# A two-block model on one core: the state space set-up with D's diagonal on TensorE and at even steps, and the state space mixer's matmuls grouped by kind

## Chip, core and metric

The kernel runs on one core of a Trainium2 chip. The metric is the device time in microseconds (us). TensorE (PE) multiplies, PEld is its weight load, VectorE (DVE), ScalarE (ACT) and GpSimd (POOL) do the rest, and SyncE (SP) issues most of the loads from HBM. ACT and POOL issue some DMAs as well, in order with their own instructions.

## What is computed

A model of two blocks on x [512 tokens, 1024 channels]. The change touches the second block: the state space mixer of its second layer, and the set-up of that mixer's factors, which is done during the feed-forward part of the layer before.

```python
# s5_mixer: 64 groups of 16 channels, each with 64 complex states
ab = exp(lr*dt) * (cos(li*dt) + 1j*sin(li*dt))       # per group and state
x[t] = ab * x[t-1] + bb @ u[t]                       # linear scan over 512 tokens
y[t] = Re(c @ x[t]) + d * u[t]                       # d: one number per channel
g_a, g_b = split(gelu(y) @ w_glu);  x_res += g_a * sigmoid(g_b)
# conv_ffn, once per layer
h = x @ w_up; h = conv_b + sum_j conv_w[j] * h[t-2+j]
x_res += (silu(h[:2816]) * h[2816:]) @ w_down
```

## The kernel before

Every large product is made of three matmuls of split fp32 operands: `lin` (L268 to L270) multiplies hi by wh, lo by wh and hi by wl. For each weight tile `wload` has SP load `w`, ACT round it to `wh` (L223) and DVE subtract to get `wl` (L224). There are three buffers of `w` and two each of `wh` and `wl`, so ACT must make the next `wh` while PE uses the present one.

**The feed-forward part, `ffn(l, ...)`.** Two halves. Each half has eleven pairs of products with w_up (loop over `j`; 24 matmuls each), whose results pass through DVE (L1995, L1999) and ACT (L1997, L2002), and then eight products with w_down (loop over `n`; 33 matmuls each). In layer 0 a generator, `s5_setup`, is advanced in between by `step(sg)`; in layer 1 there is nothing to advance. A Tile scheduler puts the instructions of each engine into order.

**The set-up, `s5_setup`.** Eight steps `q`, each for four pairs of groups, each in two parts. The first part is on POOL alone (`tt`, L1507): complex products that fill `s_bb`, `s_gr`, `s_gi`, `s_vr`, `s_vi` (512 and 576 elements per partition, two buffers each), two DMAs to `v_d`, and a table of 64 powers, `s_tab`, by six doublings of six instructions on 4 to 128 elements, sent to `tab_d` (one buffer). The second part has PE transpose `s_gr` and `s_gi` (L1570), which ACT copies to `s_w` and sends to `w_d`, and has PE multiply `s_bb` by `s_vr` and `s_vi` (L1583) into `sk`, which ACT copies to `s_k` (L1586). POOL then adds the diagonal that carries d, `s_owns` (made at L1576), to `s_k` (L1587), and ACT issues four DMAs of `s_k` to `k_d` (L1590).

**The mixer, `mixer3`.** Four steps `q` of sixteen groups. `blocks(q)` multiplies the inputs `U[q]` by `w` (from `w_d`) on PE (L1649); `states(...)` runs the scan on DVE (L1665 to L1675) with the table `tab` (from `tab_d`) and leaves `X`; `outputs(q, ...)` adds on PE, for each `e` of 8, the product of `U` with `tm` from `k_d` (L1697, all 128 rows of the array by 64 columns) and of `X` with `v` from `v_d` (L1701, 64 rows by 64 columns); `gelus` transposes (L1714) and applies the gelu. `U[0]` is first scaled by `rj` on DVE (L1642), `U[1]` to `U[3]` on POOL (L1725). `tm`, `v` and `w` share four buffers, tag `w5`, and `tab` has two; SP issues all their loads from `q` 2 on, in one queue (`factors`, L1685 and L1687, and `s5_load`, L1613 and L1615). PE's order here is that of the code. Then the products with `w_gl` begin.

## Time and profile before

| | |
|---|---|
| time, median of 3 runs | 2511.63 us (2510.29 to 2514.41) |
| the profiled execution: its time, its span | 2509.73 us, 2507.7 us |
| granted TensorE clock, mean over the span | 0.970 |
| busy: PE, DVE, ACT, POOL | 94%, 70%, 43%, 23% |
| POOL's busy time that lies within 1405 to 1830 us | 324.32 us |
| `ffn(0)` with the set-up, from its first L1995 to its last L2010 | 1457 to 1893 us |
| `mixer3` from its first L1649 to the first product with w_gl | 1946 to 2006 us |

All positions are microseconds from the span's start. A granted clock of 1.00 is 2.4 GHz and 0.50 is 1.2 GHz; a value between is a mean over a stretch. The two stretches in the last lines make up a fifth of the span, and PE is busy nearly all the time outside them.

### The profile page before, as it was taken

Reading aid. Unit: us, or ns where it says so; the run is one execution under the profiler, and the core shown is the slowest. Engines: PE = TensorE matmul, PEld = TensorE weight load, DVE = VectorE, ACT = ScalarE, POOL = GpSimd, SP = SyncE. Lnnn points to the kernel's source line nnn. Section 1 sums busy time; section 2 is a strip of 40 time slices with the busy share of each in tenths; the row PEclk is TensorE's granted clock in tenths of the full one; section 3 lists DMA queues with packets and bytes.
Section 4 is the critical chain, followed back from the end, with each engine's and each line's share of the span. In section 5 each row is a group of like instructions: output and inputs, shape, how many; then the busy total and the mean of one; then the engine's idle time right before and its main releaser. Section 6 shows DMA issues by size and latency. Waiting matters only on the chain.

```text
span 2507.7 us, 35944 instructions
## 1 busy us (share of the span) xinstructions
PE 2345.7 (94%) x13173; PEld 1909.4 (76%) x13174; DVE 1749.5 (70%) x3319; ACT 1088.4 (43%) x1706; POOL 564.5 (23%) x689
## 2 busy tenths in 40 slices
PE   7999899899999998899999987898999799999999
PEld 4666799677777776898767776686788588888887
DVE  6975668699996985777786766636657746755755
ACT  3444578434433434786345333323343234433432
POOL 0002344100000004443010599809800100000000
PEclk9999999899999998999999998998999899999999
DMA  9852688454353214896221333332346732323242
GB/s 345 294 193 88 244 316 314 166 179 133 112 176 134 97 63 144 294 334 235 88 68 62 92 112 103 104 109 97 109 145 196 208 105 93 98 85 110 94 122 97
DMA packets 136726, 385.94 MB, mean 154 GB/s; under 512 B 24632, under 2 KB 41144, under 8 KB 134496
## 3 DMA queue, kind: packets, MB, share of 16 engines
q1 hardware_dynamic: 121408, 338.51, 40.8%
q0 software_dynamic: 7488, 26.74, 3.2%
q10 hardware_dynamic: 7648, 18.32, 2.1%
q8 instruction: 108, 1.77, 0.3%
q14 instruction: 74, 0.61, 0.1%
HBM read 354.13 MB, written 29.38 MB: 153 GB/s over the span
## 4 chain that ended last, share of the span: by engine, by line
PE 35%; POOL 10%; DVE 4%; DMA 1%; issue 1%; ACT 1%; ACTq 0%; POOLq 0%; DVEq 0%; SPq 0%
PE ps L268 10%; PE ps L270 10%; PE ps L269 10%; POOL s_x L1507 3%; POOL s_tab L1507 2%; POOL s_gr L1507 1%; POOL s_gi L1507 1%; POOL s_vr L1507 1%; DVE wl L224 1%; DMA tab_d<-s_tab 1%; PE py L1701 1%; DMA w<-v_d 1%; POOL s_vi L1507 0%; POOL s_bb L1507 0%; POOL s_owns L1576 0%
## 5 line engine op out<-in xcount | busy, mean ns | idle before, releaser
L268 PE MATMUL ps<-hi,wh 128*128 128x512 f32 (+2 forms) x2248 | 903.0, 402 | 38.5 <-ACT wh L223 35.2
L270 PE MATMUL ps<-hi,wl 128*128 128x512 f32 (+2 forms) x2248 | 889.2, 396 | 9.4 <-DVE wl L224 9.4
L269 PE MATMUL ps<-lo,wh 128*128 128x512 f32 (+2 forms) x2248 | 888.0, 395 | 3.6 <-DVE lo L486 2.4
L223 ACT ACTIVATE wh<-w 128x1024 fp32r<-128x1024 f32 (+2 forms) x327 | 310.5, 951 | 620.6 <-PE ps L269 360.0
L224 DVE TENSOR_TENSOR wl<-w,wh 128x1024 fp32r<-128x1024 f32 (+3 forms) x323 | 368.3, 1140 | 275.0 <-ACT wh L223 270.8
L268 PEld LDWEIGHTS ps<-hi,wh 128*128 128x128 f32 (+1 forms) x2248 | 427.3, 190 | 144.7 <-ACT wh L223 39.2
L270 PEld LDWEIGHTS ps<-hi,wl 128*128 128x128 f32 (+1 forms) x2248 | 426.1, 190 | 114.3 <-DVE wl L224 17.8
L269 PEld LDWEIGHTS ps<-lo,wh 128*128 128x128 f32 (+1 forms) x2248 | 427.4, 190 | 97.7 <-DVE lo L486 4.4
L224 DVE TENSOR_TENSOR wl<-we,wh 128x1024 fp32r<-128x1024 f32 x128 | 169.3, 1338 | 64.8 <-ACT wh L223 60.3
L929 POOL TENSOR_TENSOR hl<-hT,hh 128x1024 fp32r<-128x1024 f32 x60 | 140.4, 2341 | 172.6 <-ACT hh L928 109.9
L223 ACT ACTIVATE wh<-we 128x1024 fp32r<-128x1024 f32 x128 | 135.3, 1059 | 52.4 <-DMA we<-in_w_ex_dram 23.0
L1999 DVE SCALAR_TENSOR_TENSOR hc<-f,cols,hc 128x511 f32<-128x511 f32 (+1 forms) x176 | 150.8, 857 | 7.0 <-ACT hc L1997 3.8
L909 PE MATMUL ps<-ht,w 128*128 128x128 f32 x1024 | 126.0, 276 | 6.7 <-ACT ht L959 6.6
L726 POOL IOTA io<- 128x512 f32 x2 | 1.1, 562 | 573.4 <-PE ps L270 573.4
L909 PEld LDWEIGHTS ps<-ht,w 128*128 128x128 f32 x1024 | 119.4, 191 | 9.4 <-ACT ht L959 9.2
L441 DVE CUSTOM_DVE_ANT_0 we<-we,crow 128x1024 f32<-128x1024 f32 x80 | 96.4, 1214 | 5.4 <-DMA we<-in_ada_t_dram 5.1
L1995 DVE TENSOR_TENSOR f<-ps,rb 128x512 f32<-128x512 f32 x88 | 60.4, 686 | 54.3 <-PE ps L270 54.0
L947 PE MATMUL pa<-wh,hh 128*128 128x256 f32 x496 | 89.3, 301 | 0.0
L223 ACT ACTIVATE hi<-hc 128x512 fp32r<-128x512 f32 x44 | 27.8, 632 | 128.4 <-DVE hc L2003 128.4
L491 DVE SCALAR_TENSOR_TENSOR x<-ps,mod,x 128x512 f32<-128x512 f32 x52 | 38.9, 748 | 59.1 <-PE ps L270 51.7
L947 PE MATMUL pa<-wl,hh 128*128 128x256 f32 x496 | 78.7, 281 | 1.5 <-DVE wl L224 1.5
L947 PE MATMUL pa<-wh,hl 128*128 128x256 f32 x496 | 79.2, 282 | 0.0
(570 smaller groups left out, 3331.0 us busy)
## 6 DMA issues: line engine op xcount, KB each, us to landing
we<-in_w_ex_dram SPq DMA_DIRECT2D x128, 512.0 KB, 6.0
w<-in_w_fu_dram SPq DMA_DIRECT2D x88, 512.0 KB, 3.5
we<-in_ada_t_dram SPq DMA_DIRECT2D x80, 512.0 KB, 5.1
w<-in_w_ex_dram SPq DMA_DIRECT2D x64, 512.0 KB, 5.6
w<-in_w_si_dram SPq DMA_DIRECT2D x48, 512.0 KB, 3.5
w<-in_w_fd_dram SPq DMA_DIRECT2D x32, 512.0 KB, 3.9
w<-in_w_ei_dram SPq DMA_DIRECT2D x20, 512.0 KB, 3.5
aw<-in_ada_w_dram SPq DMA_DIRECT2D x16, 512.0 KB, 9.1
```

The lines of the kernel that those rows point to most:

```text
L223: S.activation(hi, src, AF.Copy)
L224: eng.tensor_tensor(lo, src, hi.bitcast(F32), op=SUB)
L268: PE.matmul(ps[:m], a, h, start=(not more and k + j == 0), stop=False)
L269: PE.matmul(ps[:m], a, l, start=False, stop=False)
L270: PE.matmul(ps[:m], b, h, start=False, stop=(last and k + j == nk - 1))
L441: V.tensor_tensor_reduce(w, w, row, 1.0, 0.0, op0=MUL, op1=ADD, accum_out=st[:, n:n + 1])
L909: PE.matmul(p[:, c * 128:(c + 1) * 128], w2[:, (4 * q + c) * 128:(4 * q + c + 1) * 128], hd, start=True, stop=True)
L929: (V if e < 2 else G).tensor_tensor(hl_, win, hh.bitcast(F32), op=SUB)
L947: PE.matmul(hp[:, 0:256], h[:, 4 * n + k], w[:, k * 256:(k + 1) * 256], start=(n + i + k == 0), stop=(n + i + k == 6))
L1507: G.tensor_tensor(o, a, b, op=op)
L1995: V.tensor_tensor(t, next(up)[1], rb, op=MUL)
L1999: V.scalar_tensor_tensor(c[:, d:], t[:, :T - d], C(f"fw{l}{2 - d}", n), c[:, d:], op0=MUL, op1=ADD)
```

## The change

1. **D's diagonal.** `s_owns` is made once, for all steps, by one POOL instruction on 256 elements. PE adds it into `sk` by a product with the identity (16 columns), so ACT's copy to `s_k` is complete, and POOL's addition (L1587) is gone.
2. **Tables.** The doublings are done in the odd steps alone, for eight pairs of groups at once, on 8 to 256 elements. The third part of the table, `s_rr`, has its own tile and its own DMA in every step.
3. **Steps.** The generator is advanced once at `j` 0, twice at `j` 4 and 8 of each half, and twice after `n` 1 and 6 of each half's products with w_down, instead of at every `j` with remainder 0 or 2 by 3.
4. **Mixer.** The 16 products of `U` with `tm` of a step are made together in `within(q, tm)`, and the 32 products of `X` with `v` together in `outputs`. `within` stands ahead of the next `blocks`, and `factors` ahead of both, which moves the loads of `tm` and `v` ahead of those of `w` and `tab` on SP. The scaling of `U[1]` to `U[3]` on POOL is issued after DVE's scaling of `U[0]`.

```diff
+        owns = tl(ap, [128, 16, 16], "s_owns")
+        G.tensor_tensor(owns, own[:, None, :].to_broadcast([128, 16, 16]),
+                        C("sd", 0, 16)[:, :, None].to_broadcast([128, 16, 16]), op=MUL)
...
-            tb = tl(ap, [128, 3, 4, 64], "s_tab")
...
-            for b in range(6):
-                n = 1 << b
-                sh = [128, 4, n]
...
-            G.tensor_copy(tb[:, 2], mag[:, gq, None].to_broadcast([128, 4, 64]))
-            G.memset(tb[:, 2, :, 0:1], 0.0)
-            G.dma_start(tab_d[:, :, gq], tb)
+            if q % 2:
+                g2 = slice(4 * q - 4, 4 * q + 4)
+                tb = tl(ap, [128, 2, 8, 64], "s_tab")
...
+                for b in range(6):
+                    n = 1 << b
+                    sh = [128, 8, n]
...
+                G.dma_start(tab_d[:, 0:2, g2], tb)
+            rr = tl(ap, [128, 4, 64], "s_rr")
+            G.tensor_copy(rr, mag[:, gq, None].to_broadcast([128, 4, 64]))
+            G.memset(rr[:, :, 0:1], 0.0)
+            G.dma_start(tab_d[:, 2, gq], rr)
             yield
...
-            owns = tl(ap, [128, 2, 16], "s_owns", 2)
-            for ab in range(2):
-                G.tensor_scalar(owns[:, ab], own, C("sd", 2 * q + ab), 0.0, op0=MUL, op1=ADD)
...
-                                  m[pr, e, 0:8].rearrange("p m c -> p (m c)"), start=(a == 0), stop=(a == 1))
+                                  m[pr, e, 0:8].rearrange("p m c -> p (m c)"), start=(a == 0), stop=False)
+                PE.matmul(p[:, 0:16], ident, owns[:, 2 * q + ab], start=False, stop=True)
                 S.activation(k[:, ab], p[:, 0:128], AF.Copy)
-                G.tensor_tensor(k[:, ab, 0:16], k[:, ab, 0:16], owns[:, ab], op=ADD)
...
+            def within(q, tm):
+
+                ps = [ps_("py", 2) for _ in range(2)]
+                for e in range(8):
+                    for ab in range(2):
+                        PE.matmul(ps[e // 4][sides[ab], e % 4 * 128:e % 4 * 128 + 128], U[q][:, 8 * ab + e], tm[:, 8 * ab + e],
+                                  start=(e % 4 == 0), stop=False)
+                return ps
...
+                for h, p in enumerate(ps):
+                    for e in range(4 * h, 4 * h + 4):
+                        for a in range(2):
+                            for ab in range(2):
+                                PE.matmul(p[sides[ab], e % 4 * 128:e % 4 * 128 + 128], X[sides[ab], a, e],
+                                          v[sides[ab], e, a], start=False, stop=(a == 1 and e % 4 == 3))
...
             s0 = blocks(0)
-            for q in range(1, 4):
-                G.tensor_tensor(U[q], U[q], rj[:, None, :].to_broadcast([128, 16, 64]), op=MUL)
-            p0 = factors(0)
+            with tc.issue_after(scaled[-1]):
+                for q in range(1, 4):
+                    G.tensor_tensor(U[q], U[q], rj[:, None, :].to_broadcast([128, 16, 64]), op=MUL)
+            tm, v = factors(0)
+            X = states(*s0, gs=4)
+            y = within(0, tm)
             s1 = blocks(1)
-            X = states(*s0, gs=4)
-            o = outputs(*p0, X)
+            o = outputs(y, v, X)
             X = states(*s1)
             for q in range(2):
+                tm, v = factors(q + 1)
+                y = within(q + 1, tm)
                 s1 = blocks(q + 2)
-                p0 = factors(q + 1)
                 gelus(q, o)
-                o = outputs(*p0, X)
+                o = outputs(y, v, X)
                 X = states(*s1)
...
-                    if j % 3 == 0:
+                    if j == 0 or j % 11 in (4, 8):
                         step(sg)
-                    if j % 3 == 2 or j == 21:
-                        step(sg)
+                        if j % 11:
+                            step(sg)
...
+                    if n in (1, 6):
+                        step(sg, 2)
```

What the scheduler makes of it on ACT, at the third step of the set-up (before; `DVE`, `PE`, `Pool` and `Activation` in brackets are engines whose semaphores are waited for, `DMAHW` a load or store):

```order
L1586 ACTIVATE s_k<-sk 128x128 [waits DMAHW6_49,DMAHW1_49,DMAHW7_49,DMAHW0_49,PE_49]
L1573 DMA w_d<-s_w 128x1024 [waits Activation_49]
L1586 ACTIVATE s_k<-sk 128x128 [waits PE_49]
L223 ACTIVATE hi<-hc 128x512 [waits DVE_49]
L1590 DMA k_d<-s_k 16x2x128 [waits Pool_49]
L1590 DMA k_d<-s_k 16x2x128 x3
L223 ACTIVATE wh<-w 128x1024 [waits DMAHW5_49,PE_49]
```

And the same place of its second step after the change, where L1591 is the copy to `s_k`, L1580 the store to `w_d` and L1594 the store to `k_d`:

```order
L1591 ACTIVATE s_k<-sk 128x128 [waits DMAHW1_49,DMAHW2_49,DMAHW0_49,PE_49]
L1580 DMA w_d<-s_w 128x1024 [waits Activation_49]
L1591 ACTIVATE s_k<-sk 128x128 [waits PE_49]
L223 ACTIVATE hi<-hc 128x512 [waits DVE_49]
L1594 DMA k_d<-s_k 16x2x128 [waits Activation_49]
L1594 DMA k_d<-s_k 16x2x128 x3
L223 ACTIVATE wh<-w 128x1024 [waits DMAHW0_49,PE_49]
```

The stores stand where they stood, ahead of the next `wh`, but wait for ACT's own copy and no longer for POOL.

On PE, the first matmuls of the mixer before (U_19340 is `U[0]`, U_19348 `U[1]`, w_19449 `tm` and w_19458 `v` of step 0; a pair of the last two rows is one `e`):

```order
L1649 MATMUL ps<-U_19340,w_18931 64x64 x32
L1649 MATMUL ps<-U_19348,w_18935 64x64 x16
L1649 MATMUL pb<-U_19348,w_18935 64x64 x16
L1697 MATMUL py<-w_19449,U_19340 64x128 x2
L1701 MATMUL py<-w_19458,X 64x128 x4
L1697 MATMUL py<-w_19449,U_19340 64x128 x2
L1701 MATMUL py<-w_19458,X 64x128 x4
```

And after the change (L1655 is `blocks`, L1701 now `within`, L1712 `outputs`, L1724 the transposes; U_19174 is `U[0]`, U_19182 `U[1]`, U_19190 `U[2]`):

```order
L1655 MATMUL ps<-U_19174,w_18765 64x64 x32
L1701 MATMUL py<-w_19283,U_19174 64x128 x16
L1655 MATMUL ps<-U_19182,w_18769 64x64 x16
L1655 MATMUL pb<-U_19182,w_18769 64x64 x16
L1712 MATMUL py<-w_19292,X 64x128 x32
L1701 MATMUL py<-w_19435,U_19182 64x128 x16
L1655 MATMUL ps<-U_19190,w_19464 64x64 x32
L1724 MATMUL pm<-ident,o_19380 128x128 x8
L1712 MATMUL py<-w_19444,X 64x128 x32
```

What alternated eight times in a step now stands in one run of 16 and one of 32, and the run of 16 is ahead of the next `blocks`.

On SP, the loads for steps 1 and 2 of the mixer before (w_19601 is `w` of step 2, w_19639 `tm` and w_19648 `v` of step 1):

```order
L1613 DMA w_19601<-w_d 128x2048 [waits DMASW0_49,PE_49]
L1685 DMA w_19639<-k_d 16x16x128 [waits DMAHW1_49,DMASW2_49,PE_49]
L1615 DMA tab<-tab_d 128x3x512 [waits DMAHW2_49,DMASW1_49,DVE_49]
L1685 DMA w_19639<-k_d 16x16x128 x2
L1685 DMA w_19639<-k_d 16x16x128 [waits DMAHW5_49]
...
L1685 DMA w_19639<-k_d 16x16x128 [waits DMAHW1_49]
L1687 DMA w_19648<-v_d 128x2048 [waits DMAHW2_49,DMASW4_49,PE_49]
```

And after the change (L1691 loads `tm`, L1693 `v`, L1617 `w`, L1619 `tab`; w_19435 and w_19444 belong to step 1, w_19464 to step 2):

```order
L1691 DMA w_19435<-k_d 16x16x128 [waits DMAHW0_49,DMASW4_49,PE_49]
L1691 DMA w_19435<-k_d 16x16x128 [waits DMAHW1_49]
L1691 DMA w_19435<-k_d 16x16x128 x2
...
L1691 DMA w_19435<-k_d 16x16x128 [waits DMAHW7_49]
L1693 DMA w_19444<-v_d 128x2048 [waits DMAHW0_49,DMASW6_49,PE_49]
L1617 DMA w_19464<-w_d 128x2048 [waits DMAHW1_49,DMASW6_49,PE_49]
L1619 DMA tab<-tab_d 128x3x512 [waits DMAHW2_49,DMASW5_49,DVE_49]
```

The load of `tab`, which waits for DVE, stood ahead of seven of the eight loads of `tm` and of that of `v`; it stands behind them now.

## Rows read from the trace of the kernel before

**Rows 1.** Busy time by stretch; the third-last column is the granted clock.

```profile
1405.00:1600.00 195.00, 168.36 (x812) 133.91 (x810) 126.24 (x138) 68.31 (x95) 178.11 (x295) 0.94 0.34 105
...
1690.00:1830.00 140.00, 124.58 (x601) 99.44 (x600) 91.93 (x99) 50.19 (x73) 118.12 (x197) 0.90 0.34 108
1457.40:1893.40 436.00, 392.37 (x1889) 313.00 (x1888) 254.43 (x280) 149.07 (x212) 278.00 (x468) 0.94 0.36 111
2104.80:2457.40 352.60, 352.60 (x1560) 291.08 (x1559) 218.29 (x279) 141.65 (x179) 0.00 (x0) 1.00 0.33 102
```

**Rows 2.** Waits from 1405 to 1830: us in total, times, longest.

```profile
ACT wh L223 <- POOL s_x L1507: 65.8, 6, 14.9
...
PE ps L268 <- ACT wh L223: 35.2, 6, 10.8
```

**Rows 3.** ACT in order of time, at the third step: start, duration.

```profile
1584.61 0.28 ACT L1586 ACTIVATE s_k<-sk 128x128 f32<-128x128 f32 x1 [0.26 <-ACT s_k L1586]
...
1595.89 1.73 ACTq L1590 DMA_DIRECT2D k_d<-s_k  x4
1597.73 1.06 ACT L223 ACTIVATE wh<-w 128x1024 fp32r<-128x1024 f32 x1 [10.89 <-POOL s_x L1507]
```

**Rows 4.** POOL in order of time at the same step.

```profile
1595.63 0.22 POOL L1587 TENSOR_TENSOR s_k<-s_k,s_owns 128x16 f32<-128x16 f32 x1
```

**Rows 5.** ACT in order of time, at the seventh step.

```profile
1823.89 1.06 ACT L223 ACTIVATE wh<-w 128x1024 fp32r<-128x1024 f32 x1 [1.49 <-PE ps L269]
```

**Rows 6.** POOL's groups from 1400 to 1835; the last with its shapes apart.

```profile
L1507 POOL TENSOR_TENSOR s_x<-s_tab 128x4 f32<-128x4 f32 (+5 forms) x96 | 48.0, 500 | 6.8
L1507 POOL TENSOR_TENSOR s_tab<-s_tab 128x4 f32<-128x4 f32 (+5 forms) x96 | 41.5, 436 | 0.0
L1507 POOL TENSOR_TENSOR s_tab<-s_tab,s_x 128x4 f32<-128x4 f32 (+5 forms) x96 | 39.7, 414 | 1.2
...
L1576 POOL TENSOR_SCALAR s_owns<-s_own,cols 128x16 f32<-128x16 f32 x16 | 13.6, 861 | 0.1
...
L1507 POOL TENSOR_TENSOR s_tab<-s_tab 128x128 f32<-128x128 f32 x16 | 11.0, 688 | 0.0
```

**Rows 7.** The chain that ended last, at one step: start, duration, work.

```profile
1686.99 0.87 PE pm L1570 x8
1687.87 0.71 PE sk L1583 x32
```

**Rows 8.** The same chain in the mixer.

```profile
1962.06 5.46 DMA tab<-tab_d
1967.61 7.64 DMA w<-v_d
...
1990.52 0.58 PE py L1701 x8
1991.10 0.37 PE py L1697 x4
...
2006.24 0.43 PE ps L268
```

**Rows 9.** POOL, then DVE, in order of time as the mixer begins.

```profile
1945.52 7.93 POOL L1725 TENSOR_TENSOR U<-U,rj 128x1024 f32<-128x1024 f32 x3 [51.33 <-DVE rj L1635]
...
1945.47 3.44 DVE L1642 TENSOR_TENSOR U<-U,rj 128x512 f32<-128x512 f32 x2
...
1952.51 1.22 DVE L1667 TENSOR_TENSOR b<-b,f 128x256 f32<-128x256 f32 x1
```

**Rows 10.** DVE in order of time: ends of the scans of steps 1 and 3.

```profile
1970.82 1.26 DVE L1675 TENSOR_TENSOR X<-X,f 128x504 f32<-128x504 f32 x2
...
1985.63 0.69 DVE L1665 TENSOR_TENSOR b<-ps,tab 128x512 f32<-128x512 f32 x1 [0.96 <-PE ps L1649]
...
1996.06 1.27 DVE L1675 TENSOR_TENSOR X<-X,f 128x504 f32<-128x504 f32 x2
```

**Rows 11.** DMA issues from 1890 to 2010: KB each, median us to landing.

```profile
w<-w_d SPq DMA_DIRECT2D x2, 1024.0 KB, 9.5
```

More of the change, by code (lines that the diff above doesn't have):

```diff
@@ L1549, in s5_setup @@
                 G.dma_start(v_d[:, gq, a].rearrange("p g (m c) -> p g m c", c=16), v[:, :, 1:9])
-            tb = tl(ap, [128, 3, 4, 64], "s_tab")
-            xt = x.rearrange("p a b c -> p (a b c)").rearrange("p (a c) -> p a c", a=4)
-            G.tensor_copy(tb[:, 0, :, 0], uc[:, gq])
-            G.tensor_copy(tb[:, 1, :, 0], us[:, gq])
-            for b in range(6):
-                n = 1 << b
-                sh = [128, 4, n]
-                cmul(tb[:, 0, :, n:2 * n], tb[:, 1, :, n:2 * n], tb[:, 0, :, n - 1:n].to_broadcast(sh),
-                     tb[:, 1, :, n - 1:n].to_broadcast(sh), tb[:, 0, :, 0:n], tb[:, 1, :, 0:n], xt[:, :, 0:n])
-            G.tensor_copy(tb[:, 2], mag[:, gq, None].to_broadcast([128, 4, 64]))
-            G.memset(tb[:, 2, :, 0:1], 0.0)
-            G.dma_start(tab_d[:, :, gq], tb)
+            if q % 2:
+                g2 = slice(4 * q - 4, 4 * q + 4)
+                tb = tl(ap, [128, 2, 8, 64], "s_tab")
+                xt = x.rearrange("p a b c -> p (a b c)").rearrange("p (a c) -> p a c", a=8)
+                G.tensor_copy(tb[:, 0, :, 0], uc[:, g2])
+                G.tensor_copy(tb[:, 1, :, 0], us[:, g2])
+                for b in range(6):
+                    n = 1 << b
+                    sh = [128, 8, n]
+                    cmul(tb[:, 0, :, n:2 * n], tb[:, 1, :, n:2 * n], tb[:, 0, :, n - 1:n].to_broadcast(sh),
+                         tb[:, 1, :, n - 1:n].to_broadcast(sh), tb[:, 0, :, 0:n], tb[:, 1, :, 0:n], xt[:, :, 0:n])
+                G.dma_start(tab_d[:, 0:2, g2], tb)
[3 more added lines that the diff above has]
+            G.dma_start(tab_d[:, 2, gq], rr)
             yield
@@ L1635, in mixer3 @@
             V.tensor_copy(rj, rp[:, 0:64])
+            scaled = []
             def blocks(q):
@@ L1687, in factors, with outputs @@
                 nc.sync.dma_start(v, v_d[:, 8 * q:8 * q + 8])
-                return q, tm, v
-            def outputs(q, tm, v, X):
-                o = tl(bp, [128, 8, 8, 16], "o5", 2)
-                for e in range(8):
-                    if e % 4 == 0:
-                        p = ps_("py", 2)
-                    for ab in range(2):
-                        PE.matmul(p[sides[ab], e % 4 * 128:e % 4 * 128 + 128], U[q][:, 8 * ab + e], tm[:, 8 * ab + e],
-                                  start=True, stop=False)
-                    for a in range(2):
-                        for ab in range(2):
-                            PE.matmul(p[sides[ab], e % 4 * 128:e % 4 * 128 + 128], X[sides[ab], a, e],
-                                      v[sides[ab], e, a], start=False, stop=(a == 1))
-                    if e % 4 == 3:
-                        S.activation(o[:, :, e - 3:e + 1].rearrange("p t e c -> p e t c"),
-                                     p.rearrange("p (e t c) -> p e t c", e=4, t=8), AF.Copy)
+                return tm, v
+            def within(q, tm):
[5 more added lines that the diff above has]
+                return ps
+            def outputs(ps, v, X):
+                o = tl(bp, [128, 8, 8, 16], "o5", 2)
+                for h, p in enumerate(ps):
[4 more added lines that the diff above has]
+                                          v[sides[ab], e, a], start=False, stop=(a == 1 and e % 4 == 3))
+                    S.activation(o[:, :, 4 * h:4 * h + 4].rearrange("p t e c -> p e t c"),
+                                 p.rearrange("p (e t c) -> p e t c", e=4, t=8), AF.Copy)
                 return o
@@ L1723, in mixer3 @@
             s0 = blocks(0)
-            for q in range(1, 4):
-                G.tensor_tensor(U[q], U[q], rj[:, None, :].to_broadcast([128, 16, 64]), op=MUL)
-            p0 = factors(0)
+            with tc.issue_after(scaled[-1]):
[4 more added lines that the diff above has]
+            y = within(0, tm)
             s1 = blocks(1)
-            X = states(*s0, gs=4)
-            o = outputs(*p0, X)
+            o = outputs(y, v, X)
             X = states(*s1)
             for q in range(2):
+                tm, v = factors(q + 1)
+                y = within(q + 1, tm)
                 s1 = blocks(q + 2)
-                p0 = factors(q + 1)
                 gelus(q, o)
-                o = outputs(*p0, X)
+                o = outputs(y, v, X)
                 X = states(*s1)
-            p0 = factors(3)
+            tm, v = factors(3)
+            y = within(3, tm)
             gelus(2, o)
-            o3 = outputs(*p0, X)
+            o3 = outputs(y, v, X)
             early = []
```

2 lines of the change are left out of this document (1 added, 1 removed).

## The prediction

> **What bounds the kernel now.** I read the busy times by stretch first. TensorE is busy 94% of the span, so a gain must come from stretches where PE stands still or runs at 1.2 GHz. The change touches two such stretches.
>
> The larger one is the feed-forward part of layer 0. From its first L1995 to its last L2010 it takes 436.0 us; the same part of layer 1, with the same products and no set-up, takes 352.6 with PE never idle and the clock at 1.00 [rows 1]. Of the 83.4 us of difference, 436.0 - 392.4 = 43.6 is PE idle. Another part is the clock, 0.94 in the mean: 0.06 x 436 = 26 us of full speed that was not granted, some of it while PE stood. The set-up's own work on PE takes 0.87 + 0.71 = 1.58 us a step [rows 7], 12.6 for eight. So 43.6 idle, 12.6 work, and 27 that the low clock and small things take.
>
> The waits then say who is late. ACT waited 65.8 us, six times, for POOL before a `wh`, and PE 35.2 us, six times, for that `wh` [rows 2]. ACT in order of time shows the mechanism: the copy to `s_k` is done at 1584.89, the four stores to `k_d` are issued at 1595.89, and the next `wh` comes at 1597.73 after 10.89 us of waiting [rows 3]. The stores stand ahead of `wh` in ACT's queue and wait for POOL's addition, and POOL reaches its second addition at 1595.63 [rows 4]: 0.22 us of work, queued behind the first part of a later step. POOL is busy 178.1 of 195 us there [rows 1]. At the seventh step POOL had no such backlog, and the `wh` behind the stores waited 1.49 us, for PE [rows 5]. So the price of a step is not its work on ACT or PE but POOL's backlog, passed on through one DMA.
>
> The smaller stretch is the mixer, where the chain runs through the load of `tab` (5.46 us), the load of `v` that stands behind it on SP (7.64), and PE's `outputs` [rows 8].
>
> **The change part by part: set-up.** (1) The addition on POOL goes, and with it the wait of ACT. What remains ahead of `wh` are ACT's own copies and stores, as in [rows 5]. That is worth the idle 43.6 us if nothing else makes ACT or PE wait.
>
> (2) Does POOL keep up, so that PE doesn't wait for `s_gr` to `s_vi` instead? Its busy time in this part is 324.3 us. The table's three groups take 48.0 + 41.5 + 39.7 = 129.2 us in 288 instructions [rows 6]. The change makes 144 with twice the elements. The trace doesn't show that size. If an instruction costs the same, 65 us go; if it costs double, nothing. The largest form (128 elements) takes 0.688 against a mean of 0.436 over the six sizes of its group [rows 6], so cost grows far slower than size: I take 0.55 on average, 79 us, 50 less. `s_owns` goes from 16 instructions (13.6 us) to one, under 1. The 16 additions at 0.22 give 3.5. Four more table stores, priced by ACT's four in 1.73 [rows 3], cost 1.7. POOL is left with 324.3 - 50 - 13 - 3.5 + 1.7 = 260, or 32 a step (39 if the tables save nothing). PE takes the steps at distances that follow from layer 1: 1560 matmuls in 352.6 us are 0.226 each, so a pair is 10.9 and a product with w_down 7.5. From `j` 0 to 4 and 8 that is 43 us; from `j` 8 to `n` 1, two pairs and two products, 37; from `n` 1 to 6, 37; from `n` 6 to the next `j` 4, 62. POOL is busy from about 1405 on [rows 1], over 40 us ahead of the first pair, and needs 32 a step, so it is ahead everywhere, also with two buffers per factor. I price this at nothing; the cover is some 10 to 20 us of lead at each step.
>
> (3) The identity product adds, for each of 16 halves of a step, one product and, since `sk`'s other products are of another kind, two changes of kind. The mixer prices such a change: 8 instructions of L1701 with one change take 0.58 us, 4 of L1697 with one take 0.37 [rows 8], so 4 instructions are 0.21 and a change 0.16. Each added product is two instructions (fp32 goes in two), 0.10, and 0.32 with its changes: 16 x 0.42 = 7 at most. After the second half of a step the change back was there already, so I take 5 us; bounds 1 and 7.
>
> (4) The clock. All of the 27 us that are neither idle nor set-up could come back, or only what was lost in busy time. The rows don't divide it; clock deficits while PE stood cost nothing. I take 20; bounds 10 and 27.
>
> (5) A step now falls between products with w_down, where the next `wh` must be made while PE does the last third of a product. The order puts ACT's copies and stores (about 4 us: two of 0.28 and 1.73 in [rows 3], two larger ones and one more store) behind both tiles of the next product, so 7.5 us are there for them. I allow 3 us for small stalls over all steps.
>
> Sum for layer 0: 43.6 + 20 - 5 - 3 = 55.6, say 56. Bounds: 43.6 + 10 - 7 - 7 = 40, and 43.6 + 27 - 1 = 70, less the small pitch that layer 0 keeps, 65.
>
> **Mixer.** (6) Grouping. By the same split a step has 16 changes of kind at 0.16, and keeps two: 14 x 0.16 = 2.2 us a step, 9 in all on PE. But PE isn't alone. DVE's scans are nearly continuous: the one of step 1 ends at 1972.08, the one of step 3 runs from 1985.63 to 1997.33, 11.7 us [rows 10]. `outputs(1)` can't start before 1972; it then takes 32 x 2 x 0.0525 + 0.2 = 3.6.
>
> (7) Loads. `tm` and `v` of step 1 no longer stand behind `tab`, so PE has them in time. But `w` of step 3 now shares its buffer with `v` of step 1 (four buffers in turn, and the order of requests is another): it can be loaded only when `outputs(1)` is done, at 1975.7. A load of this size from SP landed after 9.5 us [rows 11], with others ahead of it; that of `v` took 7.64 [rows 8]. With 8 us `blocks(3)` starts at 1983.7 and its first half is done in 1.1 to 2.2, so the scan of step 3 starts at 1985 to 1986, where it started before. It ends at 1997, and the last `outputs` takes 3.6 at full clock, 7 if the pause before it takes the clock to 0.50. The products with w_gl start at 2001 to 2004, against 2006.24 [rows 8]. I take 3.5 us of gain. Bounds: a load of 5 us gives 8; one of 12 us loses 1.
>
> (8) The scaling of `U[0]` on DVE took 3.44 us for two while POOL's three took 7.93 beside it [rows 9]. Behind DVE they leave it alone, worth about 2 us at the start; then they lie over the first scan, where one addition beside POOL took 1.22 [rows 9]. The Trainium skill ("SBUF — State Buffer", Who interferes with whom) says that a DVE instruction with two SBUF inputs and a GpSimd instruction that reads SBUF exclude each other for a whole instruction, the first to start going ahead. By that, the first scan is held until POOL's last scaling ends near 1955 and the mixer loses up to 1 us here; by the rows alone it gains up to 2. I take 0, which lies between.
>
> **Sum.** 2509.7 (the profiled execution's own time; its span is 2507.7) - 56 - 3.5 = 2450.2. The median of the runs is 1.9 above that execution, so I predict **2452 us**.
>
> **Rivals.** A: the stall moves to ACT at the new places. If the copies and stores come ahead of the next `wh` at the four steps among the w_down products, PE stops about 4 us each and pays as much again at 1.2 GHz, some 28 us in all: 2480. For it: two buffers of `wh`, and a third of a product to refill. Against it: the order, and [rows 5]. B: the mixer gives nothing or loses (a load of `w` over 10 us, or the last `outputs` at low clock): 2456 to 2458. For it: the load has no other work ahead of it that would hide it. C: POOL still sets the pace, because the wide table instructions cost double beside DVE. Then POOL needs 39 a step and PE waits for the factors at the two 37 us distances of each half, 2 to 10 us each with the clock behind: about 20 to 25 us given back, 2475. Against it: the largest form's price. D, on the other side: the first loads of the next part lie in memory that the set-up frees, so SP's queue stands until the set-up's last store has landed, and the weights of that part's fourth product are behind them. The last step now comes one product (7.5 us) ahead of the end of layer 0's part. PE wants those weights three products of 5.5 us later, so there are some 10 us to spare. For the kernel to be slower than before, the set-up would have to end 60 + 10 = 70 us late, that is, POOL would have to take 330 us or more for what I price at 260. The tables at double price give 310. The change doing nothing at all is excluded by the first part: a wait that is named in the order is gone.
>
> **How the numbers follow.** This kernel's measurement tells 0.2%, 5 us, from no change. Forecast (both terms within their inner bounds, 2442 to 2465): 0.68. A: 0.12. B alone: 0.10. C: 0.06. D or anything over 2506: 0.04. The range takes the forecast, B and C's nearer half: 2441 to 2476, 0.82. Faster by over 0.2%: 0.94; within it 0.02; slower 0.04.
>
> **What would show it.** Right: in the waits of this part no ACT `wh` behind POOL, PE idle under 8 us between the first L1995's successor and the last product, clock 0.99 or more, and that part at 375 to 385 us. POOL with idle time in which it waits for PE. In the mixer, one run each of 32 and 64 PE instructions a step, the long wait before `blocks(3)` put down to the load of `w`, and the scan of step 3 starting 38 to 40 us after the mixer's first matmul. Wrong: PE waiting for `s_gr` or `s_vi` (C), `wh` late between w_down products (A), or the w_gl products starting later than 60 us after the mixer's first matmul (B).

## The result and the profile after

The changed kernel takes 2472.67 us (median of 4 runs, 2467.97 to 2477.85) against 2513.02 for the kernel before, run beside it (4 runs, 2510.29 to 2515.02). The ratio is 0.9842, 95% interval 0.9829 to 0.9856. The forecast was 2452 with a range to 2476: the sign and the range held, but 40 us came back where 59.5 were expected, and 2472.67 lies outside the forecast's own inner bounds of 2442 to 2465. The profiled execution took 2467.97 us, its span is 2466.2.

First the busy times of layer 0's feed-forward part and of layer 1's, as in [rows 1]; the third-last column is the granted clock.

```profile
1462.00:1856.60 394.60, 385.58 (x1921) 312.17 (x1920) 261.31 (x280) 150.74 (x211) 224.56 (x295) 0.99 0.38 116
2063.20:2415.80 352.60, 352.60 (x1560) 291.09 (x1559) 218.27 (x279) 141.56 (x178) 0.00 (x0) 1.00 0.33 102
```

The part went from 436.0 to 394.6 us. PE idle is 394.6 - 385.6 = 9.0 instead of 43.6, the clock 0.99 instead of 0.94. The waits of this part (us in total, times, longest), to compare with [rows 2]:

```profile
POOL s_vr L1507 <- PE sk L1587: 96.7, 5, 25.1
...
PE ps L270 <- DVE wl L224: 8.3, 6, 2.0
...
PE ps L268 <- ACT wh L223: 0.7, 1, 0.7
```

The wait of `wh` for POOL, 65.8 us before, is in this list no longer. POOL is ahead: it waited 96.7 us for PE to free its buffers. What PE still waits for is VectorE's `wl`. Now one set-up step on PE in order of time (start, duration), where the chain of [rows 7] had 0.87 and 0.71:

```profile
1511.54 0.27 PE L1577 MATMUL pm<-ident,s_gi 128*128 128x128 f32 x1
1511.74 0.42 PE L1587 MATMUL sk<-s_vr,s_bb 64*32 64x128 f32 x8
1511.98 0.40 PE L1587 MATMUL sk<-s_vi,s_bb 64*32 64x128 f32 x8
1512.31 0.39 PE L1590 MATMUL sk<-s_owns,ident 128*128 128x16 f32 x2
1512.64 0.42 PE L1587 MATMUL sk<-s_vr,s_bb 64*32 64x128 f32 x8
1512.88 0.40 PE L1587 MATMUL sk<-s_vi,s_bb 64*32 64x128 f32 x8
1513.21 0.40 PE L1590 MATMUL sk<-s_owns,ident 128*128 128x16 f32 x2
1513.45 0.48 PE L268 MATMUL ps<-hi,wh 128*128 128x512 f32 x1
```

The same view of the kernel before shows `sk` as one run of 16 and one of 16, the two halves side by side:

```profile
1687.80 0.48 PE L1583 MATMUL sk<-s_vr,s_bb 64*32 64x128 f32 x16
1688.04 0.45 PE L1583 MATMUL sk<-s_vi,s_bb 64*32 64x128 f32 x16
1688.42 0.50 PE L268 MATMUL ps<-hi,wh 128*128 128x512 f32 x1
```

From the start of the first `sk` to the next large product it was 1688.42 - 1687.80 = 0.62 us and is 1513.45 - 1511.74 = 1.71: 1.09 us more a step, 8.7 in all.

A loss that no step of the prediction names lies ahead of the part, where VectorE makes the sums of squares. DVE in order of time, then POOL:

```profile
1442.56 3.17 DVE L227 SCALAR_TENSOR_TENSOR lo<-x,cols,hi 128x512 fp32r<-128x512 f32 x1
1445.66 4.99 DVE L343 TENSOR_TENSOR acc<-acc,f 128x512 f32<-128x512 f32 x1
1450.58 0.67 DVE L1985 TENSOR_TENSOR x<-x,ps 128x512 f32<-128x512 f32 x1
```

```profile
1446.42 1.08 POOL L1507 TENSOR_TENSOR s_x<-s_pr,s_bb 128x512 f32<-128x512 f32 x1
1447.45 1.19 POOL L1507 TENSOR_TENSOR s_vi<-s_pw,s_xb 128x576 f32<-128x576 f32 x1
1448.59 1.51 POOL L1507 TENSOR_TENSOR s_gi<-s_gi,s_x 128x512 f32<-128x512 f32 x1
1450.05 0.75 POOL L1507 TENSOR_TENSOR s_xb<-s_ci,s_om 128x64 f32<-128x64 f32 x1
```

The `acc` addition takes 0.68 us when POOL's products are left out (its row in pool_light below); here it stands 5 us while POOL goes from one long product to the next. PE then waited 5.4 us for it. In the kernel before, POOL had come to the small instructions of the first step's table at this place, and `acc` was short:

```profile
1446.72 0.72 DVE L343 TENSOR_TENSOR acc<-acc,f 128x512 f32<-128x512 f32 x1
```

```profile
1446.87 0.63 POOL L1507 TENSOR_TENSOR s_x<-s_tab 128x4 f32<-128x4 f32 x1
1447.46 0.19 POOL L1507 TENSOR_TENSOR s_tab<-s_tab 128x8 f32<-128x8 f32 x1
```

In the mixer the scan of step 3 waited for `tab`, after `blocks(3)` on PE had waited 3.21 us for `w`. DVE's row, and SP's issues of `tm` and `v` of step 2 and of `w` and `tab` of step 3:

```profile
1948.47 0.69 DVE L1671 TENSOR_TENSOR b<-ps,tab 128x512 f32<-128x512 f32 x1 [1.71 <-DMA tab<-tab_d]
```

```profile
1929.81 5.88 SPq L1691 DMA_DIRECT2D w<-k_d  x8
1935.80 0.53 SPq L1693 DMA_DIRECT2D w<-v_d  x1
1936.42 0.38 SPq L1617 DMA_DIRECT2D w<-w_d  x1
1936.97 0.56 SPq L1619 DMA_DIRECT2D tab<-tab_d  x1
```

### The profile page after: what moved, and what is told of

It reads as the page before. It is cut to its first block, busy times and chain, and to the rows that moved or that the text cites. A ratio compares the mean times of both kernels' runs of the same rounds, so it can differ in the third digit from the quotient of the medians.

```text
span 2466.2 us, 35818 instructions
## 1 busy us (share of the span) xinstructions
PE 2339.5 (95%) x13205; PEld 1921.3 (78%) x13206; DVE 1764.8 (72%) x3319; ACT 1090.6 (44%) x1706; POOL 518.4 (21%) x510
## 4 chain that ended last, share of the span: by engine, by line
PE 43%; DVE 7%; ACT 1%; issue 1%; DMA 0%; ACTq 0%; DVEq 0%
PE ps L268 13%; PE ps L270 13%; PE ps L269 13%; DVE wl L224 1%; DVE hc L2013 1%; ACT wh L223 0%; DMA tab<-tab_d 0%; PE pm L372 0%; PE sk L1587 0%; PE pa L512 0%; PE pm L530 0%; PE ps L1091 0%; PE ps L1092 0%; PE po L538 0%; DVE hc L2017 0%
## 5 line engine op out<-in xcount | busy, mean ns | idle before, releaser
L270 PE MATMUL ps<-hi,wl 128*128 128x512 f32 (+2 forms) x2248 | 884.6, 394 | 8.8 <-DVE wl L224 8.8
L270 PEld LDWEIGHTS ps<-hi,wl 128*128 128x128 f32 (+1 forms) x2248 | 424.4, 189 | 109.2 <-DVE wl L224 13.8
L2009 DVE TENSOR_TENSOR f<-ps,rb 128x512 f32<-128x512 f32 x88 | 60.4, 686 | 71.2 <-PE ps L270 70.9
L491 DVE SCALAR_TENSOR_TENSOR x<-ps,mod,x 128x512 f32<-128x512 f32 x52 | 38.9, 748 | 59.0 <-PE ps L270 51.5
```

The source lines that it names most:

```text
L270: PE.matmul(ps[:m], b, h, start=False, stop=(last and k + j == nk - 1))
L491: V.scalar_tensor_tensor(xs[c], ps, mod(l, seg, c), xs[c], op0=MUL, op1=ADD)
L2009: V.tensor_tensor(t, next(up)[1], rb, op=MUL)
```

## The experiments

Twelve kernels were run. The table gives, in us of each profiled execution, four lengths worked out, to 0.1 us, from the starts and ends of rows: "ahead" is from the first product of L1951 (in the last block before layer 0's feed-forward part; its line in the kernel before, L1965 after) to the part's first `f`, the result of its first L1995 (L2009 after); "part" from there to the end of its last addition to x; "idle" is PE's in the part, by the stretch view; "mixer" from the first product of `blocks` to the first product with w_gl. The stretch between part and mixer took 52.9 to 54.5 in all of them, everything behind the mixer 501.5 to 501.8. All that lies ahead of the first L1951 product is the same code in all of them, and took 1365 to 1382: a spread that the whole time has too, so that the lengths tell more than the medians. Each length is that of one execution, and these vary as well. best_a, mix_load and mix_tab have the same code in the part, and it took 388.6, 390.5 and 393.1; the ten kernels with the mixer of after took 53.3 to 55.9 for it, the two with that of before 60.0 and 62.5. So differences under some 4.5 us in the part, or under 2.5 in the mixer, show nothing. Ratios are to the kernel before, with their 95% intervals.

| kernel | ahead | part | idle | mixer | median | ratio |
|---|---|---|---|---|---|---|
| before | 88.6 | 435.9 | 43.6 | 60.0 | 2513.0 | |
| after | 96.9 | 394.5 | 9.0 | 55.0 | 2472.7 | 0.9842 (0.9829 to 0.9856) |
| diag_only | 88.4 | 389.5 | 6.1 | 62.5 | 2472.1 | 0.9828 (0.9811 to 0.9844) |
| add_back | 96.9 | 405.4 | 20.5 | 55.5 | 2487.4 | 0.9891 (0.9874 to 0.9907) |
| no_diag | 98.7 | 387.6 | 9.7 | 55.9 | 2478.0 | 0.9846 (0.9825 to 0.9866) |
| pool_light | 88.6 | 379.7 | 0.0 | 53.6 | 2449.2 | 0.9740 (0.9724 to 0.9757) |
| even_only | 88.2 | 399.4 | 10.0 | 54.8 | 2471.9 | 0.9825 (0.9783 to 0.9866) |
| pairs_only | 98.7 | 405.4 | 14.5 | 53.3 | 2487.2 | 0.9899 (0.9877 to 0.9922) |
| best_a | 88.4 | 388.6 | 8.6 | 54.0 | 2457.7 | 0.9784 (0.9761 to 0.9807) |
| late_start | 88.1 | 409.6 | 19.1 | 55.8 | 2484.1 | 0.9889 (0.9865 to 0.9913) |
| best_dve | 88.3 | 390.7 | 11.6 | 55.8 | 2463.4 | 0.9792 (0.9767 to 0.9817) |
| mix_load | 88.4 | 390.5 | 9.0 | 60.8 | 2470.3 | 0.9837 (0.9815 to 0.9858) |
| mix_tab | 88.4 | 393.1 | 10.0 | 57.3 | 2467.8 | 0.9813 (0.9792 to 0.9834) |
| best_short | 89.8 | 397.5 | 14.6 | 54.2 | 2473.1 | 0.9838 (0.9819 to 0.9856) |

**diag_only**: the addition's removal alone, on the kernel before.

```
-                                  m[pr, e, 0:8].rearrange("p m c -> p (m c)"), start=(a == 0), stop=(a == 1))
+                                  m[pr, e, 0:8].rearrange("p m c -> p (m c)"), start=(a == 0), stop=False)
+                PE.matmul(p[:, 0:16], ident, owns[:, ab], start=False, stop=True)
                 S.activation(k[:, ab], p[:, 0:128], AF.Copy)
-                G.tensor_tensor(k[:, ab, 0:16], k[:, ab, 0:16], owns[:, ab], op=ADD)
```

> The kernel before with one edit: D's diagonal comes from the identity product on TensorE, POOL's addition is gone; tables, steps and mixer are those of before. Theory 1 (ACT's wait behind POOL's addition was the idle time, and nothing else of the change is needed to end it): layer 0's feed-forward part goes from 436 to 395 to 410 us, the mixer stays at 60, the time is 2470 to 2486 us, and no ACT wh waits behind POOL for over 2 us. Rival (the wait only moves: with 40 us of POOL work a step, PE waits for the factors instead, and the even steps are what gives the gain): the part stays at 420 us or more, the time at 2495 or more, and PE waits for s_gr to s_vi.

```profile
1470.00:1859.60 389.60, 383.54 (x1921) 309.59 (x1920) 267.59 (x280) 148.93 (x212) 292.37 (x452) 1.00 0.39 124
```

```profile
PE ps L270 <- DVE wl L224: 5.1, 8, 1.5
...
PE ps L268 <- ACT wh L223: 0.8, 1, 0.8
```

This one edit takes 46.4 us off the part, more than the whole change does (41.4), with the clock at 1.00 and all of POOL's work in place (292 us). No `wh` waits for POOL, and PE does not wait for the factors. The theory holds, and the part came out 5.5 us under the range that was given for it; the rival, that the wait moves to the factors, falls. The old mixer took 62.5 here, 2.5 over before. The median, 2472.1, is no more than 0.6 us from that of the whole change, and the intervals of the two ratios overlap: this edit alone is worth as much as all four together.

**add_back**: the changed kernel with POOL's addition again.

```
...
-                PE.matmul(p[:, 0:16], ident, owns[:, 2 * q + ab], start=False, stop=True)
...
                 S.activation(k[:, ab], p[:, 0:128], AF.Copy)
+                G.tensor_tensor(k[:, ab, 0:16], k[:, ab, 0:16], owns[:, 2 * q + ab], op=ADD)
```

> The changed kernel with one edit: no identity product, POOL adds D to s_k again as before; tables by pairs, even steps and the new mixer stay. Theory 1: the stores to k_d stand ahead of wh again and wait for POOL, so wh waits behind POOL for 2 to 11 us at most of the eight steps; the feed-forward part of layer 0 is 405 to 440 us against 394.5, the time 2480 to 2515 us. Rival (the even steps with less POOL work a step are what gives the gain, POOL reaches its addition in time): the part is 386 to 398 us, the time 2460 to 2475, no wait of wh over 2 us.

Its waits in the part:

```profile
ACT wh L223 <- POOL s_x L1507: 30.9, 4, 7.8
...
ACT wh L223 <- POOL s_gi L1507: 13.5, 2, 6.7
...
PE ps L268 <- ACT wh L223: 9.8, 6, 2.2
```

Six waits of `wh` for POOL are back, but shorter: 44.4 us in all against 65.8 in [rows 2], and PE waits 9.8 for `wh`. So less POOL work and even steps ease the same stall (part 405.4 against 435.9) without ending it. The gains of the two remedies don't add, since each takes the same idle time.

**no_diag**: the changed kernel with L1590 taken out; the term D times u is missing from its result.

> The changed kernel without the identity product and without D (the term D times u is left out of the result); nothing else differs. It prices the product. Theory 1 (the product costs 1.09 us a step, of which half because it parts the two halves of the step that ran side by side): a step takes 1.82 us on PE as in the kernel before, against 2.91, the part is 394.5 - 8.7 = 386 us and the time 2464. Rival (the price is the product and its changes of kind, 0.84 a step at most, as the prediction had it): a step takes 2.1 to 2.5 us.

A step's PE time is 1.82 us from large product to large product, as before, where after has 2.91. The part is 387.6, 6.9 less; its idle time is 0.7 higher. The price of 1.09 us a step holds; that half of it comes from parting the two halves this run can't tell, and best_a does. The median of 2478 misses the expected 2464: the stretch ahead of L1951, the same code, was 14.5 us longer in this profile than in that of after.

**pool_light**: POOL's complex products left out.

```
-                tt(re, pr, mr, MUL)
...
-                tt(im, im, x, ADD if nmi is None else SUB)
+                G.memset(re, 0.0)
+                G.memset(im, 0.0)
```

> The changed kernel with POOL's complex products of the set-up left out (each pair of results is two writes of zero), so that its state space part is not the reference's; everything else stays. It prices what POOL's work beside it costs the other engines. Theory 1 (VectorE is held by POOL's instructions): the 5 us that PE stands before the feed-forward part's first products are gone, the four waits of 2 us of L270 for wl are gone, the part is 383 to 387 us against 394.5, and the time 2472.7 - 5 - 9 - 3 = 2452 to 2460. Rival (wl is late for VectorE's own work): the waits of L270 stay, the part is 392 or more, the time 2465 or more.

```profile
1458.00:1837.80 379.80, 379.80 (x1921) 310.71 (x1920) 220.97 (x280) 153.83 (x212) 29.93 (x58) 1.00 0.36 113
```

```profile
1441.84 0.68 DVE L343 TENSOR_TENSOR acc<-acc,f 128x512 f32<-128x512 f32 x1
```

PE has no idle time at all, the stretch ahead is as short as before, and DVE is busy for 221 us instead of 261 with the same 280 instructions. The theory holds, and the gain is larger than it said: the part and the time are both 3 us under their ranges. Every stall left in after, those for `wl` too, and the 8 us ahead of the part are VectorE held by POOL. Together they cost 14.8 + 8.3 = 23 us.

**even_only** and **pairs_only** undo one half of the set-up's rearrangement each: the first makes the tables at each step, as before, the second puts the steps back to `j % 3`.

```
 even_only
-            if q % 2:
...
-                tb = tl(ap, [128, 2, 8, 64], "s_tab")
...
+            tb = tl(ap, [128, 3, 4, 64], "s_tab")
...
 pairs_only
-                    if j == 0 or j % 11 in (4, 8):
+                    if j % 3 == 0:
...
-                    if n in (1, 6):
-                        step(sg, 2)
```

> The changed kernel with one edit: the tables are made at each step by narrow instructions, as in the kernel before; identity product, even steps and the new mixer stay. Theory 2 (the wide tables, made at every second step only, put the long instructions of the second step beside the sums of squares ahead of layer 0's feed-forward part, where VectorE has no slack): from L1951's first product to the part's first f it is 88 to 89 us, as before, against 96.9 after; the part itself is 388 to 396; time 2459 to 2468 us. Rival (the start of POOL's work or the even steps do it): that stretch stays at 96 to 98, the time at 2470 or more.

> The changed kernel with one edit: steps at the places of the kernel before (j % 3); identity product, tables by pairs and the new mixer stay. Theory 2: the stretch ahead of the feed-forward part stays at 96 to 98 us, since it lies ahead of all steps; whether the part itself goes from 394.5 to 389.5, as with the identity product alone, tells if the even steps or the wide tables cost those 5 us: 388 to 391 for the steps, 393 to 397 for the tables. Time 2464 to 2475 us.

All four combinations with the identity product are then known, one execution each (the first is diag_only, which also makes `s_owns` at each step and has the old mixer):

| part (ahead) | tables at each step | tables by pairs |
|---|---|---|
| steps as before | 389.5 (88.4) | 405.4 (98.7) |
| even steps | 399.4 (88.2) | 394.5 (96.9) |

The stretch ahead follows the tables alone, as expected: 88 with narrow tables, 97 to 99 by pairs. In the part the expectations failed: even_only lies 3 us over its range, and neither alternative of pairs_only came true. With old steps the pairs cost 16 us, the even steps alone cost 10, and both together 5, which is little more than the part varies by. Both times missed their ranges as well, by 4 and 12 us. Why even steps with narrow tables leave four waits of 1.6 to 2.0 us of L270 for `wl`, where the old steps leave one of 1.5 and smaller ones, is not settled.

**late_start**: POOL's products begin behind the sums of squares.

```
...
+                z = tl(ap, [128, 1], "late")
+                V.tensor_scalar(z, rb[:, 0:1], 0.0, None, op0=MUL)
+                for s_ in (s5f[0], s5f[2], s5f[3], s5f[5]):
+                    V.tensor_scalar(s_, s_, z, None, op0=ADD)
```

> The changed kernel with one edit: what POOL's set-up reads is written once more (plus zero) by VectorE behind rb, so that POOL's products start some 55 us later, behind the sums of squares instead of beside them. Theory 1 (POOL's instructions hold VectorE there): the stretch ahead of the feed-forward part falls from 96.9 to 85 to 89 us. POOL has then about 50 us for its first step (32 us), so the part stays at 394 to 402; time 2462 to 2472 us. Rival (VectorE is late there by its own work): the stretch stays at 95 or more, and the time at 2472 or more.

The stretch ahead falls to 88.1, as the theory says. But the first step's work now lies beside the part's first products, and the part grows by 15. One row shows how:

```profile
1496.02 7.50 DVE L2018 SCALAR_TENSOR_TENSOR hc<-f,cols,hc 128x511 f32<-128x511 f32 x2
```

Two instructions of about 0.87 us in the mean (the line's group in the page of after) took 7.50, and PE then stood 5.59 us for a `wh`. The hold moved with POOL's work; it did not go away. The part lies 8 us over its range, the time 12.

**best_a**: tables and steps of before, the two halves side by side, the new mixer.

```
...
+            for a, m in ((0, vr), (1, vi)):
+                for e in range(4):
+                    for ab in range(2):
+                        pr = slice(64 * ab, 64 * ab + 64)
+                        PE.matmul(ps[ab][32 * e:32 * e + 32, 0:128],
...
+            for ab in range(2):
+                PE.matmul(ps[ab][:, 0:16], ident, owns[:, 2 * q + ab], start=False, stop=True)
```

> The changed kernel with tables and steps of the kernel before, and with the two halves of a set-up step run side by side again on TensorE, both identity products behind them. What stays of the change is the identity product and the new mixer. Theory 2 and the price of the parted halves: stretch ahead of the part 88 to 89 us, a step 1.59 + 0.45 to 0.6 = 2.0 to 2.2 us on PE against 2.68, the part 384 to 387, the mixer 55 to 56, the time 2472.7 - 8.4 - 9 = 2452 to 2460 us. Rival (a step costs what its products and changes of kind cost, whatever their order): a step 2.5 to 2.7 us, the part 389 to 391, the time 2457 to 2464.

```profile
1488.54 0.45 PE L1583 MATMUL sk<-s_vr,s_bb 64*32 64x128 f32 x16
1488.78 0.42 PE L1583 MATMUL sk<-s_vi,s_bb 64*32 64x128 f32 x16
1489.14 0.62 PE L1587 MATMUL sk<-s_owns,ident 128*128 128x16 f32 x4
1489.61 0.47 PE L268 MATMUL ps<-hi,wh 128*128 128x512 f32 x1
```

From the first `sk` to the next large product it is 1.07 us, against 1.71 after and 0.62 before. So the identity products cost 0.45 a step, 3.6 in all, and parting the halves cost 0.64, 5.1 in all. The rival's 2.5 to 2.7 us a step falls: the 1.07 stand for 2.04 in its terms. The length of the part does not show the gain: it is 388.6 against 389.5 of diag_only, over the 384 to 387 of the theory, with 2.5 us more idle, and the part varies by more than that. The time of 2457.7 lies in the ranges of both. It is the fastest here of the kernels that leave nothing out, 15 us below after; the intervals of the two do not overlap.

**best_dve**: best_a with the addition on VectorE, from PSUM.

```
...
+                V.tensor_tensor(k[:, ab, 0:16], p[:, 0:16], owns[:, 2 * q + ab], op=ADD)
+                S.activation(k[:, ab, 16:], p[:, 16:128], AF.Copy)
```

> As best_a, but D's diagonal comes neither from TensorE nor from POOL: VectorE adds it from PSUM into the first 16 columns of s_k, ScalarE copies the other 112. Theory (the wait of before came from POOL's backlog, not from the addition as such): a set-up step takes 1.59 us on PE, as before, no wh waits behind VectorE's addition for over 1.5 us, the part is 384 to 388 us against 388.6 of best_a, the time 2453 to 2460 us. Rival (the stores stand ahead of wh again, and VectorE has a queue of its own in front of the addition): wh waits 2 to 5 us at most steps, the part is 392 us or more, the time 2461 or more.

A step takes 1.59 us on PE, and no `wh` is put down to VectorE's addition: ACT's copy of the other columns waits for it, ten times, 1.3 us at the longest, 5.6 in all. That is the theory's sign and not the rival's. But idle rises from 8.6 to 11.6, the part of 390.7 lies between the two expectations, and the time of 2463.4 in the rival's range. It is not shown to be better or worse than best_a.

**mix_load** parts the mixer's two edits: products by kind, but the loads in the order of before.

```
...
+                wt = s5_load(wq, q + 2)
                 tm, v = factors(q + 1)
                 y = within(q + 1, tm)
-                s1 = blocks(q + 2)
+                s1 = blocks(q + 2, wt)
```

> As best_a, with the mixer's loads in the order of the kernel before (w and tab of step q + 2 ahead of tm and v of step q + 1), and TensorE's products by kind as after. It parts the mixer's two edits. Theory M1 (the order of loads is what the mixer gained by, since the DMA engines are some 90% busy from its start to its last loads): from the first blocks to w_gl it takes 57.5 to 62 us, as before, against 54.0 of best_a. Rival M2 (the grouping by kind gained it): 53 to 56 us.

```profile
1908.19 0.32 SPq L1615 DMA_DIRECT2D w<-w_d  x1
1910.91 0.54 SPq L1689 DMA_DIRECT2D w<-k_d  x1
1918.42 0.57 SPq L1617 DMA_DIRECT2D tab<-tab_d  x1
1919.04 4.81 SPq L1689 DMA_DIRECT2D w<-k_d  x7
```

```profile
1929.61 3.68 PE L1699 MATMUL py<-w,U 128*64 128x128 f32 x32 [7.87 <-DMA w<-k_d]
```

The mixer takes 60.8 us, as before. `tab` waits on SP for a buffer that the first scan holds (7.2 us for DVE's `X`), seven of the eight loads of `tm` stand behind it until 1919, and PE waits 7.87 us. M1 holds, though not for the reason that it gave: what these rows show is the wait in SP's queue, not busy DMA engines. The order of the loads brought the mixer's gain; grouping by kind, with that order undone, brought none. What the new order gains without the grouping no run shows.

**mix_tab**: best_a with a third buffer for `tab`, loaded ahead of `tm`.

```
...
+                tb = s5_tab(wq, q + 2)
                 tm, v = factors(q + 1)
                 y = within(q + 1, tm)
-                s1 = blocks(q + 2)
+                s1 = blocks(q + 2, tb)
```

> As best_a, with three buffers for tab and its load ahead of tm and v; w stays behind them. In the changed kernel VectorE waited 1.7 us for tab of step 3, and blocks(3) 3.2 us for w. Theory M3 (the last scan is held by whichever of w and tab lands last, and the one scan follows the other without a gap if both are there): the wait for tab goes, that for w stays or grows by 1 to 3 us since tab is ahead of it, and the mixer gains at most 1 us: 53 to 55 us against 54.0. Rival (tab is the last): 51.5 to 52.5 us.

The mixer takes 57.3, outside both ranges. VectorE no longer waits for `tab`, and PE waited 4.43 us for `w` of step 3 where it waits 2.68 in best_a, as M3 said. `blocks(3)` starts 37.0 us after the mixer's first product, against 34.2 in best_a; another 0.9 of these 2.7 us is a wait of `within(2)` for ACT's `o`. The last 0.6 of the 3.3 us are less than the mixer varies by.

**best_short**: best_a, POOL's long products in two pieces each.

```
...
+            if len(o.shape) == 4 and o.shape[2] > 7:
+                for g in range(0, 4, 2):
+                    G.tensor_tensor(o[:, g:g + 2], a[:, g:g + 2], b[:, g:g + 2], op=op)
```

> As best_a, with POOL's long products of the set-up (512 and 576 elements a partition) each cut into two of half the length. Theory (a VectorE instruction is held until POOL's instruction in front of it ends, so the length of POOL's instructions sets the hold): the longest subtraction for wl falls from 2.5 us to under 2.0, the waits of L270 for wl get shorter, idle PE in the part falls from 8.6 to 3 to 6 us and the part from 388.6 to 382 to 386; time 2450 to 2456 us. Rival (the holds add up to POOL's busy time whatever its pieces, or more pieces mean more holds): the part is 388 us or more, time 2457 or more.

DVE, then POOL, in order of time near the part's start:

```profile
1469.44 9.39 DVE L224 TENSOR_TENSOR wl<-w,wh 128x1024 fp32r<-128x1024 f32 x1 [1.04 <-ACT wh L223]
```

```profile
1469.24 1.22 POOL L1509 TENSOR_TENSOR s_x<-s_pr,s_bb 128x256 f32<-128x256 f32 x2
1470.43 1.75 POOL L1509 TENSOR_TENSOR s_gi<-s_gi,s_x 128x256 f32<-128x256 f32 x2
...
1476.22 1.53 POOL L1509 TENSOR_TENSOR s_vi<-s_vi,s_x 128x288 f32<-128x288 f32 x2
1477.70 0.81 POOL L1556 DMA_DIRECT2D v_d<-s_vr  x1
```

The theory falls: the length of one POOL instruction does not bound the hold. One `wl` took 9.39 us, while POOL ran 12 short products without a pause; it ended at 1478.83, 1.1 us after the last of them, about its own length (1.23 in pool_light). But this one hold is not the rule. Here are PE's waits in the part, and below them the first row of the same list for best_a:

```profile
PE ps L270 <- DVE wl L224: 5.3, 1, 5.3
PE pm L1577 <- POOL s_gi L1509: 3.8, 1, 3.8
PE sk L1587 <- POOL s_vi L1509: 3.6, 1, 3.6
```

```profile
PE ps L270 <- DVE wl L224: 5.6, 8, 1.5
```

One wait for `wl` took the place of eight, with nearly the same sum, and DVE is busy for 256 us in the part instead of 269. The rest of PE's idle time is waiting for POOL's factors, 9.2 us in all with 1.8 for `s_vr`; POOL's busy time in the part grew from 285 to 302 us. So the rival's numbers came true, but mostly by PE waiting for POOL.

## Why the prediction came out as it did

The stretches that the change touches lost 41.4 (part) + 4.9 (mixer) - 8.4 (ahead) = 37.9 us in the profile, where the sum had 56 + 3.5. The unchanged stretch was 3.7 us shorter in that execution.

That the range held is in part luck. It reached to 2476 because it took in rival B and the nearer half of C, and neither happened: the mixer gained, and PE never waited for POOL. What filled that part of the range was a loss that the prediction did not price. Of its signs, those of the mechanism came true: no `wh` behind POOL, POOL waiting for PE, the clock at 0.99, the scan of step 3 at 38.9 us after the mixer's first product. Those of size did not: the part was to be 375 to 385 us and is 394.6, PE's idle under 8 and is 9.0.

Step 1 (the wait of ACT goes) was right in its mechanism, as diag_only shows, and over-sized by its own rows: 43.6 us of idle time were counted as ACT's wait, but [rows 2] put only 35.2 to it. Of the rest, 8.3 us were L270 waiting for `wl`, as the group of L270 in this part of the kernel before says (busy us, mean ns, idle before):

```profile
L270 PE MATMUL ps<-hi,wl 128*128 128x512 f32 x522 | 211.6, 405 | 8.3 <-DVE wl L224 8.3
```

The same wait stands in the changed kernel with the same 8.3; pool_light shows that it is POOL beside VectorE, which the change leaves. 34.6 of the idle time came back.

Step 2 (POOL keeps up) was right, and rival C falls: POOL waits for PE. The tables take 75.9 us where 79 were estimated, all of POOL's set-up work 280 (282.5 from 1400 to 1857, less 2.6 for loads of the mixer) where 260 were. But "priced at nothing" failed: POOL ahead of PE is not POOL out of the way. This is the step that cost most: its wide tables moved the long products of the second step beside the sums of squares, 8.4 us, and pairs and even steps did not make the part shorter: it is 5 us longer than diag_only's, little more than it varies by.

The prediction looked at what POOL does to VectorE beside it for the mixer alone. The Trainium skill ("SBUF — State Buffer", Who interferes with whom) says that VectorE with two SBUF inputs and GpSimd reading SBUF block each other, and that whoever issues first has the ports for the whole instruction. The trace agrees that they block (0.68 us against 4.99 for the same addition), and goes further: the 9.39 us of best_short lie over many POOL instructions. That the first to start goes ahead these rows do not show: `acc` starts at 1445.66, the first of the long products beside it at 1446.42, and `acc` ends at 1450.65.

Step 3 (identity product): 8.7 us, outside its bounds of 1 to 7. Put behind both halves, the products and their changes of kind cost 3.6; put between them, 5.1 more. Of these 0.64 us a step 2 x 0.57 - 0.60 = 0.54 is the second half no longer running beside the first, which was not seen; the rest is more changes of kind, which were in the sum.

Step 4 (clock): what is neither idle nor set-up fell from 27.2 to 385.6 - 352.6 - 12.6 - 8.7 = 11.7 us, so 15.5 came back where 20 were taken, inside the bounds. Step 5: `wh` is late for 0.7 us only, so rival A falls; the stalls that came are those of VectorE beside POOL.

Steps 6 and 7 gave 4.9 us where 3.5 were taken. That `tm` and `v` of step 1 no longer stand behind `tab` was right, as mix_load shows. The limit that step 7 then set was not: `w` of step 3 was issued at 1936.42, ahead of the end of `outputs(1)` (1939.28), so it did not wait for that. What held it was the queue in front of it, `tm` of step 2, whose loads took SP from 1929.81 on, once `outputs(0)` had ended (1929.77). It landed after about 8 us, as estimated. The scan of step 3 began 38.9 us after the mixer's first product, where step 7 had put it, but what held it at the end was `tab` and not `blocks(3)`. The grouping's 9 us on PE gained nothing in mix_load, under the old order of loads.

Step 8: nothing moved. DVE's two scalings took 3.44 us and POOL's three 7.91, from 1908.87 on, as in [rows 9]: the changed order on POOL's queue does not make POOL wait for VectorE. The price of 0 was right for another reason.

## What to carry to other kernels

An operation between a result and its store, on an engine with a long queue, is paid by whatever stands behind the store: taking it out gave 46 us of the part here, while making the long queue shorter gave 30.5 (add_back against before) and cost 8.4 ahead of the part by moving its work. Before work of an engine off the path is priced at nothing, look which VectorE instructions lie beside it in its new place, and how long it runs there without a pause. Where small products run side by side, as the halves of `sk` here, a product of another tile belongs behind all of them, not between them.

## What was not expected of the hardware

A VectorE instruction with two SBUF inputs stood for 4.99 us (after), 7.50 for two (late_start) and 9.39 (best_short) while POOL's products followed each other without a pause, and ended just after them in the last case. With POOL's instructions cut in two the longest hold of a `wl` in the part was longer (9.39 against 2.52 in best_a), in the one execution there is. What lets VectorE in at last is not settled.

The small products of `sk` that sum over partitions 0 to 63 ran beside those over 64 to 127: all 32 instructions took 1489.14 - 1488.54 = 0.60 us in best_a, and with one half after the other each half of 16 alone took 1512.31 - 1511.74 = 0.57.
